# Rescaling a layer's normalized input in place, and three smaller edits, in a two-layer hybrid attention encoder

## The chip, the cores and the metric

The kernel runs on one core of one Trainium2 chip. A core has TensorE (PE in the profile, its weight loads PEld), VectorE (DVE), ScalarE (ACT), GpSimd (POOL) and SyncE (SP), which here only issues DMAs. They run their own instruction streams in order and wait for each other through semaphores. The metric is the device time of one execution in microseconds; the time before is the median of three runs.

## The reference

The input x is 512 tokens of 1024 numbers. Two layers follow, each of this form (D_MODEL is 1024, D_FF 2816):

```python
h = rms_norm(x, attn_norm_g[l])
proj = h @ w_in[l]
c_q, c_kv, k_rope, gq, gk, gv, pool_in, gate_logits = split_columns(proj, IN_SIZES)
o_mla = mla_branch(...)      # 8 heads of 96, low-rank q and kv
o_gqa = gqa_branch(...)      # 8 heads of 64 over 2 key/value heads
o_pool = pool_branch(...)    # centred means of windows 2, 4, 8, 16, minus the token
gates = sigmoid(gate_logits)
merged = (gates[:, :, 0] * (o_mla @ w_branch_mla[l])
          + gates[:, :, 1] * (o_gqa @ w_branch_gqa[l])
          + gates[:, :, 2] * (o_pool @ w_branch_pool[l]))
x = x + merged @ w_out[l]
hf = rms_norm(x, ffn_norm_g[l])
u = depthwise_conv(hf @ ffn_w_up[l], ...)
x = x + (silu(u_gate) * u_val) @ ffn_w_down[l]
```

`rms_norm(x, g)` is x times one factor of the token, 1/sqrt(mean(x*x) + eps), times one gain of the column. The attention branches normalize queries and keys per head once more, and take a softmax over 512 keys.

## The kernel before

**Layout.** The residual stream lies transposed in SBUF: `XM[:, kc]` holds 128 features (partitions) by 512 tokens, kc from 0 to 7. Each float32 matrix product is made of three float32r products (`mm3`, L396): every operand is kept as a high half (the number rounded to float32r) and a low half (what the rounding lost), and PE adds hi·hi, hi·lo and lo·hi in a PSUM bank. There are eight PSUM banks, handed out by tag: "acc", "S", "ST", "AV", "mi" (`ps`, `free`, L310 and L325).

**The normalized input.** `HH` and `HL` are the halves of x times the gain, *without* the token's factor. The norm's sums are made beside other work; `norm_finish` (L492) turns them into the token factors in two forms: `rt`, one number per partition for results whose partitions are tokens, and `rbc`, a 128x512 tile with the factor of each token along the free axis, for results whose partitions are features. Every product of HH and HL is scaled by one of them on the way out of PSUM.

**Order of a layer.** `tok_major` (L598) makes products with tokens on the partitions: four banks, one for each 128 tokens; for each kc one weight piece, 12 matmuls. `feat_major` (L615) makes products with features on the partitions, one bank, 24 matmuls for two weight pieces. A layer runs:
1. the MLA latents (`tok_major`, 384 columns), then the four groups of pool channels (`feat_major`), whose windowed sums run on POOL and DVE beside the next stages;
2. the GQA query projection (`tok_major(gqb, T)`, L772) into the banks `qtags` = AV, AV, mi, ST. Its results are squared by ACT (`gq_square`) and rotated by DVE (`gq_rope`, L786: three products from PSUM, the last into `gqr`, then the bank is free; the sum of the two parts is an addition of POOL's into `gqr`);
3. the projection of GQA keys, values and the MLA rotary key (`tok_major(kvb, 288, pool_product)`, L830). Ahead of its kc = 4, `pool_product` (L815) puts the four pool products into the same four banks `qtags`. `gk_evac` (L834) and `kv_evac` (L856) then take the results out, with ACT's `scale=rtok(b)` and DVE's product with `rtok(b)`;
4. GQA attention, with the gates and branch products of the pool branch and then of the GQA branch (`gates`, L902) put between the heads' matmuls as filler;
5. MLA attention, with the rest of the GQA and the MLA branches' gates and products as filler;
6. the output projection, the feed-forward layer (norm factor `rbc` on DVE, convolution on ACT and DVE), the down projection.

**Gates.** `gate(m)` makes 128 gate logits with `feat_major`; DVE multiplies the bank by `rbc` into a tile `gt` and frees the bank (`logits`), then ACT takes tanh(0.5 x) of that tile in place. `product` makes (tanh + 1) times the branch's bank; the merged sum gathers in XM.

**MLA softmax.** For a head, `a_part` (L1303) makes the four 128x512 blocks of scores of the leading halves and takes the maximum over each block's keys, in groups of 32 lanes (`largest`); `over_keys` takes it over the four blocks. The maxima of the four groups of 32 partitions then have to meet on one group: `gather` copies three 32x16 pieces there, from other partitions, into the tile `nmt`; `over_groups` reduces the four to `mrow`, negated; `row` multiplies it by a piece of the identity into 32 rows of `qb`, so that the next matmuls with `qb` as the moving operand (`b_part`, L1339) subtract each query's maximum inside PSUM. ACT's exponential follows, then its halves `ph` (ACT or DVE) and `pl` (DVE), and the products with the values.

**Weights.** SP streams the weights in 512 KB transfers into `raw`. `w_split` (L344) halves each piece of up to 512 columns: ACT copies to the high half, then the low half is raw minus high, on DVE for the first eight pieces, on POOL for the next three, and else on whichever `pick` (L367) finds earlier, with a bias of 2.54 us against DVE. The halves are made three pieces ahead of use (`LA`), in six buffers each.

**What sets the order.** All engines' programs are written out in an order that a planner inside the kernel decides at build time: `Clock` (L134 on) keeps a modelled time for PE and for each engine, `at` and `chain` put steps into a heap by modelled time, `done` and `need` carry the modelled due times, and the `Engine` wrappers (L215 on, the lines under which nearly all instructions of ACT, DVE and POOL are recorded) add each operation's modelled cost. So an added or a dearer operation can also shift the place of others. `low` lets a step of DVE give way for up to a given time while DVE has a backlog. On the chip each engine runs its list in that order, and a bank or buffer is waited for where the planner had expected it free.

The names of the profile: XM, HH, HL, `raw`, `wh`/`wl` (weight halves), `gqr` (rotated GQA queries), `gt` (gate tile), `nmt`, `mrow`, `qb` as above; `mxh` a pool group's mixed input; `kh` and `q` halves of keys and queries; `a`, `u` tiles of the feed-forward layer; `ps_TAG` a PSUM bank.

Of the kernel before, what the change touches and what calls it, by code (L numbers as in the profile page):

```python
# [18 lines left out]
P = 128  # L19
# [195 lines left out]
class Engine:  # L215
# [31 lines left out]

    def tensor_reduce(self, out, in_, *a, **k):
        self._two(in_)
        return self.eng.tensor_reduce(out, in_, *a, **k)  # L250

    def tensor_scalar(self, out, *a):
# [21 lines left out]
def trunk(ctx: ExitStack, tc: tile.TileContext, x, w, prm, gb, cst, pad, out):  # L274
# [57 lines left out]
    pieces, swidth = _stream()  # L332
    soff = np.concatenate([[0], np.cumsum(swidth)]) * P
    st = {"dma": 0, "split": 0, "use": 0}
    raws, halves = {}, {}

    def w_dma():
        i = st["dma"]
# [5 lines left out]
    def w_split():  # L344
        j = st["split"]
        sl, off, wd = pieces[j]
        while st["dma"] <= sl:
            w_dma()
        r = raws[sl][:, off:off + wd]
        hi = hlp.tile([P, T], F32R, tag="wh", name=f"wh{j}")  # L350
        lo = hlp.tile([P, T], F32R, tag="wl", name=f"wl{j}")
        ck.fin = ck.now
        if j == 0:
            V.tensor_copy(hi[:, :wd], r)
        else:
            A.activation(hi[:, :wd], r, AF.Copy)
        e = V if j < KC else G if j < KC + 3 else pick(W_BIAS, ck.fin + ck.SEM)
        ck.free[e.kind] = max(ck.free.get(e.kind, 0.0), ck.fin + ck.SEM)
        e.tensor_tensor(lo[:, :wd], r, f(hi[:, :wd]), ALU.subtract)
        done("w", j)  # L360
        if j + 1 == len(pieces) or pieces[j + 1][0] > sl:

            at(max(0.0, ck.free[e.kind] - ck.now) + D_FREE, lambda: w_upto(sl + 1 + RAW))
        halves[j] = (hi, lo)
        st["split"] += 1
# [193 lines left out]
    def layer(l, sq, xsrc):  # L559
# [35 lines left out]
            chain(([("rt", G1)], tables), after=20.0)  # L595


        def tok_major(banks, wd, between=None):  # L598
            for kc in range(KC):
                if between and kc == 4:  # L600
                    between()
                wh, wl = wnext()
                need(("H", G1, kc))
                if st["use"] <= 2:
                    late = ((HH, wl), (HL, wh)) if kc == 0 else ((HL, wh), (HH, wl))
                    for n, (x_, w_) in enumerate(((HH, wh), *late)):
                        for b in range(4):
                            mm(banks[b][:, :wd], x_[:, kc, b * P:b * P + P], w_[:, :wd], n == 0 and kc == 0, False)
                    continue
                for b in range(4):  # L610
                    bs = slice(b * P, b * P + P)
                    mm3(banks[b][:, :wd], HH[:, kc, bs], HL[:, kc, bs], wh[:, :wd], wl[:, :wd],
                        kc == 0, kc == KC - 1)

        def feat_major(acc, gen):  # L615

            for kc in range(KC):
                if kc:
                    yield
                if kc % 4 == 0:  # L620
                    wh, wl = wnext()
                need(("H", gen, kc))
                ws = slice((kc % 4) * P, (kc % 4) * P + P)
                mm3(acc, wh[:, ws], wl[:, ws], HH[:, kc, :], HL[:, kc, :], kc == 0, kc == KC - 1)

# [143 lines left out]
        at(0.5, set_keys)  # L769

        at(14.0, set_ones)
        tok_major(gqb, T)  # L772
        gqo = [slot("gqr") for _ in range(4)]

        def gq_square(b):
# [51 lines left out]

        ktags = ("acc", "acc", "S", "ST")
        kvb = [ps(t) for t in ktags]
        tok_major(kvb, 288, pool_product)  # L830
        gkn, kj, gk1 = slot("gkn"), slot("kj"), slot("gk1")
        krt = small("krt", [P, 4, 32], bufs=1)

        def gk_evac():  # L834
            for b in range(4):
                A.activation(gkn[:, b * P:b * P + P], kvb[b][:, 0:P], AF.Copy, scale=rtok(b))
            chain(*rope_steps(heads(gk1), heads(gkn), *(
                bc(tabs[1][:, o:o + 256].rearrange("p (b f) -> p b f", b=4)[:, :, None, :], [P, 4, 2, 64])
                for o in (0, 256)), [P, 4, 2, 64], 32, V), lambda: done("gkr", l), after=ck.fin - ck.now)
# [16 lines left out]
        def kv_evac(b):  # L856
            vh, v0 = VG[b]
            src = kvb[b][:, P:2 * P].rearrange("p (h f) -> p h f", f=64)
            A.activation(vh[:, :, 0:64], src, AF.Copy, scale=rtok(b))
            A.activation(krt[:, b, :], kvb[b][:, 2 * P:288], AF.Copy, scale=rtok(b))  # L860

            def lo():
                V.scalar_tensor_tensor(vh[:, :, 65:P], src[:, :, 1:64], rtok(b), f(vh[:, :, 1:64]), ALU.mult,
                                       ALU.subtract)
                V.scalar_tensor_tensor(v0, src[:, :, 0], rtok(b), f(vh[:, :, 0]), ALU.mult, ALU.subtract)
                free(ktags[b])
                done("vg", l, b)
            chain(lo, after=ck.fin - ck.now + 0.1)
# [33 lines left out]
        def gates(br, okey, odst, mode):  # L902
            hold = {}

            def gate(m):
                tag = "AV" if br == 2 and m < 2 else "acc"
                acc = ps(tag)
                yield from feat_major(acc, G1)
                t = hold[m] = slot("gt")

                def logits():
                    V.tensor_tensor(t[:, :T], acc, nrm["rbc"][:, :T], ALU.mult)
                    free(tag)

                chain(([("rbc", G1)], way(br, logits, 1.0)), lambda: A.activation(t[:, :T], t[:, :T], AF.Tanh, scale=0.5))

            def branch(m):
                acc = ps("acc")
# [248 lines left out]
        def attention(kind, fill, okey, odst):  # L1167
# [135 lines left out]
            def a_part(h, k):  # L1303
# [18 lines left out]
                def gather():  # L1322
                    for g in range(4):
                        if 32 * g != base:
                            V.tensor_copy(s["pk"][base:base + 32, g if g < 3 else base // 32], s["pk"][32 * g:32 * g + 32, 3])

                def over_groups():
                    V.tensor_reduce(s["row"][base:base + 32], s["pk"][base:base + 32].rearrange("p g j -> p j g"), AX.X, ALU.max,
# [283 lines left out]
        fb.upto(PRE_B)  # L1612
        while not ck.has(("tq", l, 0)) and fb.step():
            pass
        now_mla[0] = True
        attention("mla", fb, "om", omla)
        rest[0].finish()


        sq = slot("sq")  # L1620
# [307 lines left out]
```

## Time and profile before

| | |
|---|---|
| three runs | 1571.52 us median (1571.37 to 1576.09) |
| the profiled execution | 1572.05 us |
| its span (first to last instruction) | 1570.3 us |
| granted TensorE clock, mean | 0.999 |
| DMA | 166.46 MB, 106 GB/s on average |

The profile is of one execution. "Busy" is the time in which an engine executed instructions, as a share of the span or of a named stretch; semaphores and the issuing of DMAs do not count. In rows of groups, `out<-in 128x512 fp32r<-128x512 f32 x32` is the written and the read tile with their shapes and types and the number of instructions; numbers like `742/751/753` are the shortest, median and longest duration in ns; `| 15.3, 852 | 0.4` is the sum in us, the mean in ns, and the idle time of the engine just ahead of them. A row of a single instruction starts with its start time and its duration in us. A row of waits names the instruction that waited, behind the arrow the instruction that released it, and then the sum of the waits, their number and the longest, in us.

The layers' stages lie about here: GQA query projection at 44 to 66 us in the first layer and 826 to 848 in the second, the key/value projection right behind, GQA attention 130 to 240 (first layer), MLA attention 240 to 340 and 1020 to 1120, the output projection behind each of these, and the feed-forward layer with its evacuations `u` from about 443 us in the first layer; the down projection is last.

### The profile page before, as it was taken

Reading aid. Unit: us, or ns where it says so; the run is one execution under the profiler, and the core shown is the slowest. Engines: PE = TensorE matmul, PEld = TensorE weight load, DVE = VectorE, ACT = ScalarE, POOL = GpSimd, SP = SyncE. Lnnn points to the kernel's source line nnn. Section 1 sums busy time; section 2 is a strip of 40 time slices with the busy share of each in tenths; the row PEclk is TensorE's granted clock in tenths of the full one; section 3 lists DMA queues with packets and bytes.
Section 4 is the critical chain, followed back from the end, with each engine's and each line's share of the span. In section 5 each row is a group of like instructions: output and inputs, shape, how many; then the busy total and the mean of one; then the engine's idle time right before and its main releaser. Section 6 shows DMA issues by size and latency. Waiting matters only on the chain. (4 is left out here: it accounts for less than half of the span.)

```text
span 1570.3 us, 20451 instructions
## 1 busy us (share of the span) xinstructions
PE 1548.3 (99%) x7034; PEld 1288.0 (82%) x7034; DVE 1008.8 (64%) x1471; ACT 788.6 (50%) x1460; POOL 1032.4 (66%) x918
## 2 busy tenths in 40 slices
PE   9999999899999999999999999999999999999999
PEld 8878787778888888888898888877788888888888
DVE  6778889996267777711046788899862777776000
ACT  6557866664444444432244687756533444444221
POOL 4866986655667666654578669767546766666542
PEclk9999999999999999999999999999999999999999
DMA  5432234324323223333335222433252232332331
GB/s 201 126 113 74 75 111 141 101 91 136 106 94 100 100 97 94 94 120 109 114 106 135 93 79 70 147 116 112 69 157 98 86 102 94 96 100 99 108 129 46
DMA packets 82855, 166.46 MB, mean 106 GB/s; under 512 B 20928, under 2 KB 42944, under 8 KB 82752
## 3 DMA queue, kind: packets, MB, share of 16 engines
q1 hardware_dynamic: 82464, 165.03, 34.1%
q8 instruction: 55, 0.90, 0.2%
q14 instruction: 48, 0.39, 0.1%
q10 hardware_dynamic: 288, 0.14, 0.0%
HBM read 151.50 MB, written 13.63 MB: 105 GB/s over the span
## 5 line engine op out<-in xcount | busy, mean ns | idle before, releaser
L242 POOL TENSOR_TENSOR wl<-raw,wh 128x512 fp32r<-128x512 f32 (+2 forms) x499 | 671.0, 1356 | 356.5 <-ACT wh L235 331.6
L235 ACT ACTIVATE wh<-raw 128x512 fp32r<-128x512 f32 (+2 forms) x521 | 309.1, 607 | 122.7 <-PE ps_ST L389 41.3
L246 DVE SCALAR_TENSOR_TENSOR a<-u,prm,a 128x511 f32<-128x511 f32 x176 | 246.4, 1401 | 93.0 <-ACT a L235 86.1
L389 PE MATMUL ps_acc<-HH,wl 128*128 128x512 f32 x592 | 230.9, 390 | 0.4 <-POOL wl L242 0.4
L389 PE MATMUL ps_acc<-HH,wh 128*128 128x512 f32 x592 | 231.3, 391 | 0.0
L389 PE MATMUL ps_acc<-HL,wh 128*128 128x512 f32 x592 | 230.9, 390 | 0.0
L389 PEld LDWEIGHTS ps_acc<-HH,wl 128*128 128x128 f32 x592 | 111.3, 188 | 24.3 <-POOL wl L242 0.9
L389 PEld LDWEIGHTS ps_acc<-HH,wh 128*128 128x128 f32 x592 | 111.5, 188 | 22.9 <-issue 0.3
L389 PEld LDWEIGHTS ps_acc<-HL,wh 128*128 128x128 f32 x592 | 111.4, 188 | 22.9
L242 POOL TENSOR_TENSOR al<-a,ah 128x512 fp32r<-128x512 f32 x44 | 57.8, 1314 | 84.9 <-ACT ah L235 84.9
L389 PE MATMUL ps_AV<-HH,wh 128*128 128x512 f32 x288 | 112.3, 390 | 0.0
L389 PE MATMUL ps_AV<-HH,wl 128*128 128x512 f32 x288 | 112.1, 389 | 0.0
L389 PE MATMUL ps_AV<-HL,wh 128*128 128x512 f32 x288 | 112.1, 389 | 0.0
L389 PE MATMUL ps_ST<-HH,wh 128*128 128x512 f32 x240 | 93.5, 390 | 0.0
L389 PE MATMUL ps_ST<-HL,wh 128*128 128x512 f32 x240 | 93.4, 389 | 0.0
L389 PE MATMUL ps_ST<-HH,wl 128*128 128x512 f32 x240 | 93.4, 389 | 0.0
L235 ACT ACTIVATE ah<-a 128x512 fp32r<-128x512 f32 x44 | 27.8, 632 | 127.1 <-DVE a L242 127.1
L235 ACT ACTIVATE a<-a 128x512 f32<-128x512 f32 x44 | 27.8, 633 | 110.0 <-DVE a L246 110.0
L235 ACT ACTIVATE a<-u,prm 128x512 f32<-128x512 f32 x88 | 70.9, 808 | 20.8 <-DVE u L242 20.6
L235 ACT ACTIVATE HH<-XM,prm 128x512 fp32r<-128x512 f32 x32 | 23.1, 722 | 101.6 <-DVE XM L242 53.9
L235 ACT ACTIVATE gt<-gt 128x512 f32<-128x512 f32 x48 | 30.2, 630 | 75.5 <-DVE gt L242 73.3
L389 PEld LDWEIGHTS ps_AV<-HH,wl 128*128 128x128 f32 x288 | 54.1, 188 | 11.3
(415 smaller groups left out, 3798.4 us busy)
## 6 DMA issues: line engine op xcount, KB each, us to landing
raw<-w SPq DMA_DIRECT2D x228, 512.0 KB, 3.5
raw<-w SPq DMA_DIRECT2D x13, 384.0 KB, 3.0
XM<-x SPq DMA_DIRECT2D x16, 256.0 KB, 3.4
dtq<-tr SPq DMA_DIRECT2D x16, 192.0 KB, 1.9
dtk<-tr SPq DMA_DIRECT2D x16, 192.0 KB, 2.3
tf<-dtq SPq DMA_DIRECT2D x48, 64.0 KB, 2.3
tf<-dtk SPq DMA_DIRECT2D x48, 64.0 KB, 2.1
raw<-w SPq DMA_DIRECT2D x6, 448.0 KB, 3.4
```

Of the source, the lines that this page charges most:

```text
L235: return self.eng.activation(out, in_, func, **k)
L242: return self.eng.tensor_tensor(out, *a)
L246: return self.eng.scalar_tensor_tensor(out, *a)
L389: PE.matmul(o, lhsT=lhsT, rhs=rhs, start=start, stop=stop)
```

## The change

There are four edits.

- **The input gets the token factor in place.** `tok_major` takes a function that it calls behind each kc. During the GQA query projection it is `rescale(kc)`: once PE's 12 matmuls of that kc are issued, DVE makes hs = XM x gain x `rbc` (a new tile), ACT rounds hs into HH, and DVE puts hs - HH into HL, over the old halves. The key/value projection and the gates read these (`scaled=True` makes them wait for the "scaled" halves). `gk_evac` and `kv_evac` lose their factor.
- **The gates' tanh reads PSUM.** `logits` is gone; ACT takes tanh(0.5 x) straight from the bank into `gt` and the bank is freed behind that.
- **The shifted copies become reductions.** `gather` takes the maximum over an axis of one element instead of a copy. The planner's cost of a reduction with such a short axis (up to 4) grows by 0.08 us.
- **Weights' low halves.** During MLA attention `pick` is not asked; all low halves go to POOL.

```diff
     def tensor_reduce(self, out, in_, *a, **k):
         self._two(in_)
+        if in_.shape[-1] <= 4:
+            self.ck.took(self.kind, 0.08)
         return self.eng.tensor_reduce(out, in_, *a, **k)
...
-        e = V if j < KC else G if j < KC + 3 else pick(W_BIAS, ck.fin + ck.SEM)
+        e = V if j < KC else G if j < KC + 3 or pool_only[0] else pick(W_BIAS, ck.fin + ck.SEM)
...
-        def tok_major(banks, wd, between=None):
+        def tok_major(banks, wd, between=None, scaled=False, then=None):
...
-                need(("H", G1, kc))
+                need(("H", G1, kc, "scaled") if scaled else ("H", G1, kc))
...
+                if then:
+                    then(kc)
...
-        tok_major(gqb, T)
+        def rescale(kc):
+            hs_ = slot("hs")[:, :T]
+
+            def lo():
+                V.tensor_tensor(HL[:, kc], hs_, f(HH[:, kc]), ALU.subtract)
+                done("H", G1, kc, "scaled")
+
+            chain(([("rbc", G1)], lambda: V.scalar_tensor_tensor(
+                hs_, XM[:, kc], col(PRM_AG + kc), nrm["rbc"][:, :T], ALU.mult, ALU.mult)),
+                  lambda: A.activation(HH[:, kc], hs_, AF.Copy), lo, after=0.3)
+
+        tok_major(gqb, T, then=rescale)
...
-        tok_major(kvb, 288, pool_product)
+        tok_major(kvb, 288, pool_product, scaled=True)
...
-                A.activation(gkn[:, b * P:b * P + P], kvb[b][:, 0:P], AF.Copy, scale=rtok(b))
+                A.activation(gkn[:, b * P:b * P + P], kvb[b][:, 0:P], AF.Copy)
...
-            A.activation(vh[:, :, 0:64], src, AF.Copy, scale=rtok(b))
-            A.activation(krt[:, b, :], kvb[b][:, 2 * P:288], AF.Copy, scale=rtok(b))
+            A.activation(vh[:, :, 0:64], src, AF.Copy)
+            A.activation(krt[:, b, :], kvb[b][:, 2 * P:288], AF.Copy)
...
-                V.scalar_tensor_tensor(vh[:, :, 65:P], src[:, :, 1:64], rtok(b), f(vh[:, :, 1:64]), ALU.mult,
-                                       ALU.subtract)
-                V.scalar_tensor_tensor(v0, src[:, :, 0], rtok(b), f(vh[:, :, 0]), ALU.mult, ALU.subtract)
+                V.tensor_tensor(vh[:, :, 65:P], src[:, :, 1:64], f(vh[:, :, 1:64]), ALU.subtract)
+                V.tensor_tensor(v0, src[:, :, 0], f(vh[:, :, 0]), ALU.subtract)
...
-                yield from feat_major(acc, G1)
+                yield from feat_major(acc, G1, scaled=True)
                 t = hold[m] = slot("gt")
 
-                def logits():
-                    V.tensor_tensor(t[:, :T], acc, nrm["rbc"][:, :T], ALU.mult)
+                def squash():
+                    A.activation(t[:, :T], acc, AF.Tanh, scale=0.5)
                     free(tag)
 
-                chain(([("rbc", G1)], way(br, logits, 1.0)), lambda: A.activation(t[:, :T], t[:, :T], AF.Tanh, scale=0.5))
+                chain(squash)
...
-                            V.tensor_copy(s["pk"][base:base + 32, g if g < 3 else base // 32], s["pk"][32 * g:32 * g + 32, 3])
+                            V.tensor_reduce(s["pk"][base:base + 32, g if g < 3 else base // 32],
+                                            s["pk"][32 * g:32 * g + 32, 3].unsqueeze(2), AX.X, ALU.max)
...
-        now_mla[0] = True
+        now_mla[0] = pool_only[0] = True
         attention("mla", fb, "om", omla)
         rest[0].finish()
+        pool_only[0] = False
```

In instructions: PE's are the same in number, and in the same order up to GQA attention. DVE gets 16 hs and 16 HL, loses the 48 products of the gates, has 48 reductions in place of the copies, and eight instead of thirteen of the weights' 512-column low halves; POOL has five more of these. ACT gets 16 copies into HH. SP's transfers are the same in number and order.

More of the change, by code (lines that the diff above doesn't have):

```diff
@@ L334, in trunk @@
     st = {"dma": 0, "split": 0, "use": 0}
-    raws, halves = {}, {}
+    raws, halves, pool_only = {}, {}, [False]
     def w_dma():
@@ L613, in tok_major, with feat_major @@
                         kc == 0, kc == KC - 1)
-        def feat_major(acc, gen):
+                if then:
+                    then(kc)
+        def feat_major(acc, gen, scaled=False):
             for kc in range(KC):
@@ L621, in feat_major @@
                     wh, wl = wnext()
-                need(("H", gen, kc))
+                need(("H", gen, kc, "scaled") if scaled else ("H", gen, kc))
                 ws = slice((kc % 4) * P, (kc % 4) * P + P)
```

## The prediction

> **What bounds the kernel now.** I read the page's busy table first, then waits of PE, then stretches of 20 to 100 us, then single instructions.
>
> ```profile
> span 1570.3 us, 20451 instructions
> ...
> PE 1548.3 (99%) x7034; PEld 1288.0 (82%) x7034; DVE 1008.8 (64%) x1471; ACT 788.6 (50%) x1460; POOL 1032.4 (66%) x918
> ```
>
> TensorE (PE) is the bound: 22 us of the span are not matmul time, and the change leaves every matmul in place. So only PE's waits can be won, and every new one is lost in full. The profiled execution took 1572.05 us, 1.75 around its span and 0.03% over the median of 1571.52; the sum below starts from 1572.05.
>
> ```profile
> 240.00:340.00 100.00, 93.17 (x401) 74.13 (x400) 98.10 (x162) 61.82 (x116) 65.91 (x56) 1.00 0.37 111
> 340.00:440.00 100.00, 100.00 (x443) 82.64 (x442) 48.47 (x68) 44.13 (x79) 57.84 (x45) 1.00 0.38 116
> 1020.00:1120.00 100.00, 92.19 (x391) 73.84 (x391) 97.67 (x159) 58.44 (x110) 66.26 (x55) 0.98 0.35 107
> 1100.00:1120.00 20.00, 18.10 (x73) 14.50 (x72) 18.93 (x30) 9.77 (x19) 11.26 (x11) 0.91 0.23 75
> 44.00:66.00 22.00, 22.00 (x98) 17.94 (x97) 10.95 (x22) 8.95 (x20) 18.94 (x18) 1.00 0.64 155
> 826.00:848.00 22.00, 22.00 (x100) 18.29 (x99) 10.97 (x21) 6.88 (x14) 17.41 (x19) 1.00 0.61 150
> 57.96:68.33 10.37, 10.34 (x52) 8.46 (x51) 6.29 (x12) 6.09 (x13) 7.53 (x7) 1.00 0.65 137
> 834.58:847.84 13.26, 13.26 (x61) 11.00 (x60) 5.54 (x13) 6.72 (x14) 9.47 (x9) 1.00 0.64 144
> 130.00:240.00 110.00, 108.80 (x501) 89.71 (x501) 96.11 (x179) 82.12 (x161) 86.97 (x117) 1.00 0.31 93
> ```
>
> Columns: stretch, length, busy time and count of PE, PEld, DVE, ACT, POOL, granted clock, DMA. The first and third rows are MLA attention of the two layers. There DVE is 98% busy and PE issues 401 and 391 matmuls per 100 us against 443 at full rate (second row): 42 and 52 missing, 9.5 and 11.7 us, together 21.2. The fourth row shows a part of it: a granted clock of 0.91 over 20 us, 1.8 us.
>
> ```profile
> PE ps_ST L1348 <- DVE qb L242: 6.8, 4, 1.9
> PE ps_AV L1348 <- DVE qb L242: 4.8, 4, 1.9
> ...
> PE ps_S L393 <- ACT gt L235: 1.1, 1, 1.1
> ```
>
> PE's longest waits are for qb, the row of negated maxima. One of them, by DVE, POOL and PE:
>
> ```profile
> 1086.35 3.46 DVE L258 COPY nmt<-nmt 32x16 f32<-32x16 f32 x3
> 1089.85 0.26 DVE L250 TENSOR_REDUCE mrow<-nmt 32x16 f32<-32x64 f32 x1
> 1090.21 0.69 DVE L242 TENSOR_TENSOR qb<-mrow,C 32x512 fp32r<-32x512 f32 x1
> ...
> 1088.50 1.28 POOL L242 TENSOR_TENSOR wl<-raw,wh 128x512 fp32r<-128x512 f32 x1
> ...
> 1090.95 0.50 PE L1348 MATMUL ps_ST<-qb,kh 128*128 128x512 f32 x1 [1.84 <-DVE qb L242]
> ```
>
> Three copies of 16 elements take 3.46 us and end (1089.81) when POOL's subtraction ends (1089.78); a reduction of 64 elements takes 0.26. PE stands 1.84 us behind them.
>
> **Part 1, MLA attention: copies, gates, weights.**
>
> ```profile
> L258 DVE COPY nmt<-nmt 32x16 f32<-32x16 f32 x18 | 15.3, 852 | 0.4
> ...
> L242 DVE TENSOR_TENSOR gt<-ps_acc,rbc 128x512 f32<-128x512 f32 x7 | 4.7, 675 | 0.0
> ...
> L242 DVE TENSOR_TENSOR wl<-raw,wh 128x512 fp32r<-128x512 f32 x2 | 2.4, 1178 | 0.1
> ```
>
> (DVE, 240 to 340 us.) A reduction over one element replaces each copy. None of 32x16 inputs is in the trace; its price lies between 0 and the 0.26 of the four times larger one; I take 0.26. DVE then sheds 18 x (0.852 - 0.26) = 10.7, all gates' products 4.7 and the weights' halves 2.4: from 98.1 to about 80 us. A head's chain to qb shrinks by 3 x 0.59 = 1.8 on average, by 2.7 in the case shown, as much as PE waits there. What is late next is the usual exp and its halves, which filler matmuls cover. I take **-20** of the 21.2; bounds -10 (half stays) and -21.
>
> The weights' halves that leave DVE (five of 512 in the program) cost POOL 1.3 us each; POOL is at 66% there: 0, and 1.3 each if a weight is just due.
>
> **Part 2, gates.** The tanh reads the accumulator; 48 DVE products vanish.
>
> ```profile
> L235 ACT ACTIVATE gt<-gt 128x512 f32<-128x512 f32 x48 | 30.2, 630 | 75.5 <-DVE gt L242 73.3
> ```
>
> ACT keeps 48 instructions of about this length; reading PSUM instead of SBUF is not shown for tanh, so I keep 0.63. The accumulator is now freed by ACT instead of DVE. Behind a tanh that waits stand exponentials and weights' halves, for which PE waits; ACT is 62% busy in MLA, 82 of 110 us in GQA (last row of stretches), so 0, and 0.63 for a gate if ACT is late. GQA has 1.2 us of PE idle; with DVE lighter I take **-1** (0 to -1.2).
>
> **Part 3, the rescale.** Per layer and per kc it adds hs (DVE, from XM and rbc), a copy to HH (ACT), HL (DVE). Per layer 16 DVE and 8 ACT instructions enter beside the GQA projection. No transfer is added, and SP keeps its order.
>
> ```profile
> L246 DVE SCALAR_TENSOR_TENSOR HL<-XM,prm,HH x32: 742/751/753, 4.9 to 1208.3; 128x512 fp32r<-128x512 f32 x32
> ...
> L242 DVE TENSOR_TENSOR XM<-XM,gt x16: 692/1084/1796, 366.2 to 1165.7; 128x512 f32<-128x512 f32 x16
> L242 DVE TENSOR_TENSOR mgl<-XM,mgh x16: 691/692/694, 367.6 to 1168.2; 128x512 fp32r<-128x512 f32 x16
> ```
>
> Alone, hs costs 0.75 and HL 0.69, mean 0.72. With two operands in SBUF, an addition can take up to 1.80. What waits is queued behind them: the rope of the GQA queries, which frees the four PSUM banks of the pool products, which PE issues in the middle of the next projection. In the changed program's order seven HL and five hs come between the first layer's 57.96 us and its first rope (68.33), two more before the last rope; in the second layer 13 between 834.58 and 847.84, then two.
>
> ```profile
> 73.38 0.68 DVE L242 TENSOR_TENSOR gqr<-ps_ST,tabg 128x512 f32<-128x512 f32 x1
> ...
> 74.67 0.39 PE L389 MATMUL ps_ST<-mxh,wh 128*128 128x512 f32 x1
> ...
> 852.89 0.68 DVE L242 TENSOR_TENSOR gqr<-ps_ST,tabg 128x512 f32<-128x512 f32 x1
> ...
> 855.94 0.39 PE L389 MATMUL ps_ST<-mxh,wh 128*128 128x512 f32 x1
> ```
>
> The last bank is freed 0.61 us (74.67 - 74.06) and 2.37 us before PE takes it. DVE's idle time in the two stretches is 10.37 - 6.29 = 4.08 and 13.26 - 5.54 = 7.72. First layer: 14 x 0.72 - 4.08 - 0.61 = 5.4 late. Second: 15 x 0.72 - 7.72 - 2.37 = 0.7. Floor: **6.1**.
>
> Above it comes POOL, busy 18.94 and 17.41 of 22 us, 83%. Some seven of the new instructions of a layer meet it; afterwards POOL's next instruction is the addition into gqr, which waits for the rope. A random arrival waits half of a subtraction: 0.83 x 0.65 = 0.54, 14 times 7.6. DVE's wait for ACT's copy between hs and HL (0.63) is spent in the same gaps. I take 6.1 + 7.6 = **+14**; bounds 6 and 24 (each of the 14 waits for all 1.29 of a subtraction: 18.1).
>
> The Trainium skill, "SBUF — State Buffer", section "Who interferes with whom", says that a DVE instruction with two SBUF inputs and a GpSimd instruction that reads SBUF block each other for the whole instruction, and that a reduction never contends on trn2. The additions of up to 1.80 agree, the reductions of 0.26 too; by the full block the term would be the upper bound, the first rival.
>
> PE's 1.1 us wait in the first layer (ps_S, listed under ACT) falls behind the new one: **-1**. The other edits (evacuations without a factor) swap forms of one length: 0.
>
> **Sum:** -20 - 1 - 1 + 14 = -8: 1572.05 - 8 = **1564 us**, 0.5% under the median.
>
> **The rivals.**
>
> *Lock-step in the GQA projection (slower).* DVE and POOL alternate, each new instruction pays a whole subtraction, weights come late too: 24. PE's standstills then cost clock as in the row with 0.91, 1.8 us a layer: 27.8. Sum -22 + 27.8 = +6: 1578. It outweighs the gain from a term of 22, a wait of (22 - 6.1) / 14 = 1.14 us each. For it: POOL's share, and additions at 1.80. Against it: POOL runs out of work before the rope.
>
> The skill's "TensorE: Matmul & The Clock Gate", "Part 1: The HAM clock gate", has half clock after an idle window of about 3.4 us; one standstill per layer of 5 us or more would bring it.
>
> *No contention.* The new instructions fall between POOL's: 6 instead of 14, 1556. Against it: 83%.
>
> *MLA is not cleared.* The replaced copies wait as before, or another wait takes their place (ACT's copies, kh from DMA): gain 10 instead of 20: 1574. Against it: 0.26 for a reduction beside POOL, and DVE's fall to 80%.
>
> **How the numbers follow.** Chances: forecast 0.44 (own range 1557 to 1570), lock-step 0.38, no contention 0.10, MLA not cleared 0.08. About 0.3%, 4.7 us, is what a measurement can tell from no change: 1566.8 to 1576.2 is "same". Faster: 0.34 of the forecast and 0.10; same: 0.10 of it, 0.08, and 0.02 of lock-step; slower: 0.36. The range runs from 1553 (no contention, all of MLA and GQA cleared) to 1583 (lock-step with 15 of the 20 won).
>
> **What would show it.** Right: nmt reductions under 0.3 us beside POOL, MLA stretches with 440 matmuls per 100 us and DVE near 80%, PE idle before the pool products of 5 to 9 us a layer, released by DVE gqr. Wrong: no idle there, or over 11 us a layer with a granted clock under 1; waits for qb that stay; a new wait of PE for an accumulator that ACT holds.

## The result and the profile after

The changed kernel takes 1583.57 us, median of five runs (1581.72 to 1585.15), against 1571.37 for the kernel before (five runs in all): a ratio of 1.0076, 95% interval 1.0057 to 1.0096. It is 12 us slower, where 1564 and a gain of 8 had been forecast; the time lies 0.6 us over the top of the range. The profiled execution, 1585.15 us, has a span of 1583.4 us, 13.1 over that of before.

From the page of the changed kernel:

```profile
span 1583.4 us, 20454 instructions
...
PE 1554.8 (98%) x7034; PEld 1293.4 (82%) x7034; DVE 986.6 (62%) x1447; ACT 797.8 (50%) x1480; POOL 1045.2 (66%) x922
```

DVE is lighter by 22 us, and PE waits more. Where it waits is in the stretches of the changed kernel (stretch, length, busy time and count of PE, PEld, DVE, ACT, POOL, granted clock, DMA):

```profile
240.00:340.00 100.00, 100.00 (x445) 82.91 (x444) 90.44 (x171) 66.80 (x126) 78.02 (x68) 1.00 0.47 137
1020.00:1120.00 100.00, 100.00 (x448) 82.99 (x447) 90.09 (x171) 67.77 (x128) 79.54 (x68) 1.00 0.47 143
...
130.00:240.00 110.00, 106.19 (x484) 86.77 (x483) 86.84 (x154) 84.16 (x166) 86.15 (x118) 1.00 0.23 73
920.00:1020.00 100.00, 96.01 (x436) 78.03 (x435) 77.92 (x138) 77.20 (x151) 77.16 (x105) 1.00 0.23 69
60.00:80.00 20.00, 14.73 (x74) 11.30 (x73) 17.99 (x28) 9.61 (x18) 8.59 (x8) 1.00 0.35 86
80.00:100.00 20.00, 16.84 (x83) 14.38 (x82) 19.38 (x37) 11.47 (x31) 15.79 (x15) 0.83 0.32 99
848.00:880.00 32.00, 25.29 (x127) 21.02 (x126) 29.20 (x49) 17.32 (x33) 22.85 (x20) 0.89 0.31 88
```

MLA attention (first two rows) is clear: PE is busy all of the time, with 445 and 448 matmuls per 100 us. GQA attention (next two) is not: 3.8 and 4.0 us without a matmul, where the first had 1.2 before. The projections (last three) lose most: PE is busy 14.73 of 20 us, and behind that its granted clock is 0.83.

The waits of PE in the changed kernel (released by, sum, times, longest):

```profile
PE ps_acc L391 <- POOL wl L242: 4.8, 8, 0.7
PE ps_S L391 <- DVE nm L252: 2.9, 2, 1.5
PE ps_acc L391 <- DVE vm L242: 2.7, 2, 1.4
PE ps_AV L391 <- DVE gqr L242: 2.6, 2, 1.3
PE ps_mi L391 <- DVE gqr L242: 2.0, 2, 1.0
PE ps_acc L391 <- ACT wh L235: 1.8, 2, 1.3
PE ps_ST L391 <- POOL qb L242: 1.8, 4, 0.7
PE ps_ST L391 <- ACT oph L235: 1.7, 2, 0.9
PE ps_AV L391 <- ACT wh L235: 1.4, 1, 1.4
...
PE ps_AV L391 <- POOL wl L242: 0.9, 1, 0.9
```

DVE's qb, the longest wait before, is gone. In its place stand the weights' halves (wl and wh, 8.9 us in all), the ropes' banks (gqr, and the last of the four, listed under oph, 6.3 us), and in GQA attention nm, vm and POOL's qb.

For the comparisons below the waits are added up by stage, so that half clock and restarts count too: for each matmul, the distance to the start of the next one minus the median distance for its shape (0.227 us for 512 columns). This is worked out from the matmuls' starts in each trace; the sums are us of one profiled execution, "1" and "2" are the layers, and stages are cut at the same places of PE's work. A 0 stands for -0.2 to 0.1. GQA attention here begins right behind the projections; the "3 and 1 us" of the expectations are for 130 to 240 us and 920 to 1020 us alone.

```
                                     span  projections    GQA att.      MLA att.
                                             1     2       1     2       1     2
before                             1570.3   0.6   0.3     5.7   1.0     9.5  11.6
after                              1583.4  14.2  11.8     7.4   7.7     0     0
e1  no rescale, no gates' edit     1553.1   0.6   0.2     4.4   1.9     2.1   2.1
e2  gates' edit, no rescale        1559.1   0.6   0.5     8.9   6.9     0     0
e3  rescale, no gates' edit        1574.5  11.6  10.5     3.3   1.0     2.1   3.7
e4  after, no copy to HH           1578.8  11.8   9.1     7.4   7.9     0     0
e5  after, POOL quiet              1559.9   2.6   1.8     7.1   6.9     0     0
e6  after, rescale in kv           1582.9   6.0  13.0    15.2   7.0     0     0
e7  e2 in the order of e1          1557.5   0.6   0.2     5.5   2.9     3.3   3.3
e8  reductions alone               1562.4   0.6   0.5     4.5   1.0     7.1   6.9
e9  after, GQA's halves on POOL    1570.6  11.8   9.8     3.7   3.3     0     0
e10 e1 with more filler            1549.6   0.6   0.5     4.5   1.0     0.5   0.6
e11 MLA's halves on POOL alone     1569.5   0.6   0.3     4.4   1.0    10.8  10.8
e12 e9, no rescale                 1550.6   0.6   0.5     3.8   3.3     0     0
```

After minus before: -21.3 in MLA attention (the prediction's first term said -20), +25.1 in the projections (+14), +8.4 in GQA attention (-2 for the gates and the keys' wait together), 0.8 at the start.

### The profile page after: what moved, and what is told of

It is laid out like the page before. It is cut to its first block, busy times and chain, and to the rows that moved or that the text cites. A ratio compares the mean times of both kernels' runs of the same rounds, so it can differ in the third digit from the quotient of the medians.

```text
span 1583.4 us, 20454 instructions
## 1 busy us (share of the span) xinstructions
PE 1554.8 (98%) x7034; PEld 1293.4 (82%) x7034; DVE 986.6 (62%) x1447; ACT 797.8 (50%) x1480; POOL 1045.2 (66%) x922
## 4 chain that ended last, share of the span: by engine, by line
PE 86%; DVE 4%; POOL 4%; ACT 3%; issue 2%; DMA 1%; SPq 0%; POOLq 0%; DVEq 0%; ACTq 0%
PE ps_acc L391 40%; PE ps_AV L391 21%; PE ps_ST L391 19%; PE ps_S L391 2%; PE ps_mi L391 2%; POOL wl L242 1%; DVE hs L246 1%; PE ps_ST L1363 1%; POOL oraw L242 1%; DMA XM<-x 1%; DVE wl L242 1%; ACT wh L235 1%; POOL qa L242 0%; PE ps_ST L1321 0%; DMA raw<-w 0%
## 5 line engine op out<-in xcount | busy, mean ns | idle before, releaser
L242 POOL TENSOR_TENSOR wl<-raw,wh 128x512 fp32r<-128x512 f32 (+2 forms) x503 | 678.0, 1360 | 398.4 <-ACT wh L235 361.2
L235 ACT ACTIVATE ah<-a 128x512 fp32r<-128x512 f32 x44 | 27.8, 632 | 129.1 <-DVE a L242 129.1
L235 ACT ACTIVATE a<-a 128x512 f32<-128x512 f32 x44 | 27.8, 632 | 105.6 <-DVE a L246 105.5
L391 PEld LDWEIGHTS ps_AV<-HH,wh 128*128 128x128 f32 x288 | 54.1, 188 | 11.5 <-DVE sq L242 0.4
```

The costliest lines, as they stand in the source:

```text
L235: return self.eng.activation(out, in_, func, **k)
L242: return self.eng.tensor_tensor(out, *a)
L391: PE.matmul(o, lhsT=lhsT, rhs=rhs, start=start, stop=stop)
```

## The experiments

Four kernels first crossed the two doubtful edits, with the reductions and the weights' rule in all of them: neither the rescale nor the gates' edit (e1), the gates' edit alone (e2), the rescale alone (e3), both (the changed kernel). The programs of PE are equal in e1 and e3, and in e2 and the changed kernel, so that the rescale can be read off without a change of order.

**e1**: the changed kernel without `rescale`, with the gates' `logits` and the evacuations' factors as before.

```diff
+            V.tensor_reduce(s["pk"][base:base + 32, g if g < 3 else base // 32],
+                            s["pk"][32 * g:32 * g + 32, 3].unsqueeze(2), AX.X, ALU.max)
...
+        e = V if j < KC else G if j < KC + 3 or pool_only[0] else pick(W_BIAS, ck.fin + ck.SEM)
```

> The kernel before with the two edits of MLA attention alone: reductions in place of the shifted copies, all low halves of the weights on POOL there. No rescale; the gates' logits stay a DVE product. Theory P (the prediction's sum): these two edits win -20 in MLA attention and nothing else moves, 1571.4 - 20 = 1551 us, and PE's lost time in GQA attention (130 to 240 us and 920 to 1020 us) stays at 3 and 1 us as before. Rival (the whole gain needs the lighter DVE of the gates as well): 1558 or more, with waits for qb of over 5 us left.

Measured: 1555.23 us (1554.72 to 1557.40) beside 1570.12 for the kernel before, ratio 0.9907 (0.9892 to 0.9922). The two small edits win 15 us; the waits for qb are gone, GQA attention is as before. The 4 us that are missing to 1551 are at the end of each MLA stage, a wait for `vt`, which e8 and e10 take up.

**e2**: e1 with the gates' tanh from PSUM; HH and HL unscaled.

```diff
-                def logits():
-                    V.tensor_tensor(t[:, :T], acc, nrm["rbc"][:, :T], ALU.mult)
+                def squash():
+                    A.activation(t[:, :T], acc, AF.Tanh, scale=0.5)
                     free(tag)
```

> e1 plus the gates' tanh from PSUM, with HH and HL left unscaled: the token factor is left out of the gates' logits. PE's program is that of the changed kernel, without the rescale's instructions. Theory P (tanh from PSUM costs nothing; the GQA attention's new loss of 10.7 us comes from the lateness that the rescale brings): 1550 us, GQA attention as in e1. Theory Q (the loss belongs to the gates' edit: the planner's other order of PE, DVE and ACT, with the tanh in ACT's queue): 1551 + 10 = 1561 us, with the waits for DVE nm and DVE vm in GQA attention also here.

**e3**: the changed kernel with the gates' `logits` back on DVE, as in the kernel before.

> The changed kernel with the gates' logits on DVE as before: they are multiplied by the token factor a second time. PE's program is that of e1. Theory P: as the changed kernel, 1583, the GQA attention's loss of 10 us is here too. Theory Q: 1583.6 - 10 = 1573 us, GQA attention at 3 and 1 us lost as in e1, the projection's 11 us per layer unchanged.

Measured: e2 1559.25 us (1558.92 to 1560.85), ratio 0.9929 (0.9913 to 0.9946); e3 1576.72 (1576.29 to 1578.06), ratio 1.0043 (1.0028 to 1.0058); same chip as e1. Theory Q holds and P falls: the loss of GQA attention is in e2, without any rescale, and not in e3, with all of it. The edits' prices nearly add: the rescale costs 1576.7 - 1555.2 = 21.5 us, the gates' edit 1559.3 - 1555.2 = 4.0, so 1580.7 with both, where the ratio of the changed kernel, 1.0076, gives 1582.1 on this chip. The 4.0 are a balance: by the table e2 loses 9.5 us more than e1 in GQA attention, and wins back e1's 4.2 in MLA attention.

**e4**: the rescale without ACT's copy.

```diff
-                  lambda: A.activation(HH[:, kc], hs_, AF.Copy), lo, after=0.3)
+                  lo, after=0.3)
```

> The changed kernel without ACT's copies of hs into HH (the high halves stay unscaled, the low halves are hs minus those). DVE's instructions are all there; ACT never waits for hs, and the weights' high halves aren't queued behind such a wait; DVE doesn't wait for ACT between hs and HL. Theory A (the DVE instructions alone, each waiting for POOL, make the ropes late and PE waits for the pool products' banks): PE's loss in the two projections stays at 11 to 12 us a layer, 1582 to 1584, now all of it ahead of the pool products. Theory B (ACT's in-order queue: HH waits for hs and the next weights' halves stand behind it): the loss falls to 6 us a layer or less, 1573 or less, and the waits for wh and wl at 63 to 79 us are gone.

Measured: 1580.59 us (1580.37 to 1580.83), ratio 1.0066 (1.0051 to 1.0081). The waits of PE in e4:

```profile
PE ps_AV L391 <- DVE gqr L242: 4.8, 4, 2.6
...
PE ps_mi L391 <- DVE gqr L242: 3.1, 2, 1.6
...
PE ps_acc L391 <- ACT wh L235: 2.0, 2, 1.1
...
PE ps_acc L391 <- POOL wl L242: 1.2, 2, 0.6
```

With the shorter waits, which are not listed here, those for weights shrink from 8.9 to 3.6 us, and those for the ropes' banks grow from 6.3 to 8.4: the projections lose 11.8 and 9.1 us instead of 14.2 and 11.8. ACT's queue decides for the most part where PE stands, and for a smaller part how long. That is theory A in the main (its time was put at 1582 or more, and not all of the waiting stands at the ropes), with some 2.5 us a layer for B.

**e5**: POOL's subtractions of the two projections' weights become memsets.

```diff
+        if e is G and 16 <= j % PER < 33:
+            G._two(lo[:, :wd])
+            nc.gpsimd.memset(f(lo[:, :wd]), 0.0)
+        else:
             e.tensor_tensor(lo[:, :wd], r, f(hi[:, :wd]), ALU.subtract)
```

> The changed kernel, but the low halves of the GQA and key/value projections' weights (pieces 16 to 32 of each layer) are set to zero by a POOL memset in the place of the subtraction; that part of these products is left out. The programs of PE, DVE and ACT are those of the changed kernel. Theory K (DVE's instructions with two SBUF operands wait for POOL's subtractions): hs falls from a mean of 1.41 us to under 1.0, HL to 0.7, and PE's loss in the two projections from 14 and 12 us to under 6 each, 1570 or less. Theory L (32 more instructions are too many for DVE's gaps whatever POOL does, and DVE and ACT wait for each other): hs gets shorter, but 9 us or more a layer stay, 1576 or more.

Measured: 1561.69 us in one run, beside 1572.74 for the kernel before on that chip. DVE's new instructions in the changed kernel, then in e5 (shortest, median, longest in ns):

```profile
L246 DVE SCALAR_TENSOR_TENSOR hs<-XM,prm,rbc x16: 740/1285/1793, 50.7 to 864.8; 128x512 f32<-128x512 f32 x16
L242 DVE TENSOR_TENSOR HL<-hs,HH x16: 674/692/1779, 58.6 to 867.7; 128x512 fp32r<-128x512 f32 x16
```

```profile
L246 DVE SCALAR_TENSOR_TENSOR hs<-XM,prm,rbc x16: 740/746/1555, 49.0 to 844.8; 128x512 f32<-128x512 f32 x16
```

Theory K: with POOL's reads of SBUF out of the way hs takes 0.75 us instead of 1.29 in the median, the projections lose 2.6 and 1.8 us, and with the same 32 instructions of DVE the rescale costs 2 to 3 us in all (e5 against e2: 1561.7 to 1559.3 on different chips, 4.4 to 1.1 us lost in the projections). The Trainium skill, "SBUF — State Buffer", section "Who interferes with whom", says that a DVE instruction with two SBUF inputs contends with a GpSimd instruction that reads SBUF and not with one that only writes it. The memsets agree with it: the median of 0.75 is that of an undisturbed instruction. The price belongs to the two together: POOL's subtractions without the rescale (e2) lose 0.6 and 0.5 us in the projections, the rescale without the subtractions 2.6 and 1.8, both 14.2 and 11.8. What e5 can't tell apart is DVE's relief from that of PE, for which the memsets also come earlier than the subtractions.

**e6**: the rescale one stage later, behind the key/value projection's kc, which reads the unscaled halves again.

```diff
-        tok_major(gqb, T, then=rescale)
+        tok_major(gqb, T)
...
-        tok_major(kvb, 288, pool_product, scaled=True)
+        tok_major(kvb, 288, pool_product, then=rescale)
```

> The changed kernel with the rescale one stage later: behind each kc of the key/value projection, which again reads the unscaled halves and has its token factors at the evacuations. Same number of instructions (the evacuations' forms apart). Theory N (the price is DVE time in a stretch where DVE is full, wherever it is put between the query projection and the gates): the ropes are in time, but the keys' evacuation and the first gates come late, the loss is as large, 1580 or more. Theory M (the price comes from the ropes that free the pool products' banks, and from the weights' halves of the short pieces): the loss in both projections falls to under 5 us a layer, 1570 or less.

Measured: 1586.02 us (1584.65 to 1588.55), ratio 1.0079 (1.0054 to 1.0104): theory N. The longest waits of PE in e6:

```profile
PE ps_AV L391 <- DVE HL L242: 11.4, 2, 5.7
PE ps_ST L391 <- DVE gqr L242: 6.2, 2, 3.6
```

Moved off the query projection, the rescale is waited for by the first gate, 5.7 us in each layer (in the table this wait is counted with GQA attention in the first layer, with the projections in the second). The ropes are not in time either, as theory N had them: their last bank is waited for 3.6 and 2.6 us. A place a stage later is no cheaper.

**e7**: e2, but the planner goes on counting a DVE product per gate, so that PE and POOL have the programs of e1.

```diff
                 def logits():
-                    V.tensor_tensor(t[:, :T], acc, nrm["rbc"][:, :T], ALU.mult)
+                    V._two(t[:, :T])
                     free(tag)
...
-                chain(([("rbc", G1)], way(br, logits, 1.0)), lambda: A.activation(t[:, :T], t[:, :T], AF.Tanh, scale=0.5))
+                chain(([("rbc", G1)], way(br, logits, 1.0)), lambda: A.activation(t[:, :T], acc, AF.Tanh, scale=0.5))
```

> e2 with the planner's books left as they were: it still counts a DVE product for each gate and frees the modelled bank behind it, but the product isn't issued and tanh reads PSUM (the token factor is left out of the gates). PE's and POOL's programs are those of e1. Theory O (the 4 us of e2 over e1 come from the order that the planner writes for GQA attention): as e1 or slightly faster, 1553 to 1556, PE's loss in GQA attention 3 and 1 us. Theory Q2 (a tanh in ACT's queue that holds the bank is dear by itself): 1558 or more, with waits for a bank that ACT holds.

Measured: 1558.98 us (1558.05 to 1559.33) beside 1572.74, ratio 0.9902 (0.9876 to 0.9928), which includes e1's 0.9907. For GQA attention theory O holds in the main: 5.5 and 2.9 us, near e1's 4.4 and 1.9 and not e2's 8.9 and 6.9. The time itself is undecided, since 3.3 us are lost in each MLA stage, against 2.1 in e1. Part of that is a wait for the branch's product (first row). The sign of theory Q2 is there too, but small: PE waits twice in GQA attention, 1.1 us in all, for a bank that ACT's tanh holds (second row).

```profile
PE ps_acc L391 <- DVE gt L246: 2.9, 2, 1.4
...
PE ps_acc L391 <- ACT gt L235: 1.1, 2, 0.7
```

**e8** and **e11**: the two small edits apart. e8 is the kernel before with the reductions only, e11 with the weights' rule only.

> The kernel before with the reductions in place of the shifted copies alone; weights in MLA attention go where the planner puts them. If the copies were the whole of MLA's loss: 1555 as e1, the wait for vt of 1.4 us at the end of each MLA stage perhaps gone. If the low halves on POOL are needed as well: 1560 or more, with waits for qb or weights left in MLA attention.

> The kernel before with the weights' low halves in MLA attention on POOL alone, copies as before. If the copies that wait for POOL hold PE up, relieving DVE of five low halves wins nothing: 1570 to 1572, the waits for qb stay at 13 us. If DVE's load was the cause: 1566 or less.

Measured: e8 1563.40 us (1562.29 to 1564.56) beside 1572.74, ratio 0.9931 (0.9904 to 0.9958); e11 1574.04 (1571.30 to 1577.56) beside 1572.05, ratio 1.0009 (1.0000 to 1.0019). The waits of PE in e8, then in e11:

```profile
PE ps_AV L391 <- DVE vt L246: 3.5, 2, 1.7
...
PE ps_ST L1351 <- DVE qb L242: 0.2, 1, 0.2
```

```profile
PE ps_AV L1348 <- DVE qb L242: 5.9, 4, 2.3
PE ps_acc L389 <- DVE gt L246: 3.8, 4, 1.9
PE ps_S L1348 <- DVE qb L242: 2.8, 3, 2.0
```

e11 is as its first theory said in the main: relief of DVE's load alone wins nothing. (Its waits for qb come to 10 us and not to 13, with longer ones for gt.) e8 met neither expectation: the copies were all of the waits for qb (0.2 us are left), but the time is at 1563, with a new loss at the end of each MLA stage. PE's program suggests why: between the last head's scores and its last product there are 21 filler matmuls in the kernel before, 9 in e1 and none in e8.

**e10**: e1 with more of the MLA branch's gates as filler.

```diff
-SOONER = {1: 3 * KC, 0: 6 * KC}
+SOONER = {1: 3 * KC, 0: 52}
```

> e1 with 52 instead of 48 units of the MLA branch's gates as filler in MLA attention; the same work in another place. In e1 9 filler matmuls are left between the last head's scores and its last product, 21 in the kernel before; here it is 24. If the 1.7 us that e1 loses at the end of each MLA stage are filler that ran out: 1555.2 - 3.4 = 1552, the wait for vt gone. If the filler is missed elsewhere: 1555 or more.

Measured: 1551.72 us (1551.39 to 1553.97) beside 1572.05, ratio 0.9872 (0.9855 to 0.9888). The losses at the stage's end are gone, so in e1 they were filler that ran out; for e8 the same is likely, but no run gave it more filler. This is the fastest kernel of the study, 1.3% faster than the one before and, by the two ratios, 2.0% faster than the changed one. From its page:

```profile
PE 1542.4 (100%) x7034; PEld 1287.8 (83%) x7034; DVE 983.7 (63%) x1469; ACT 789.0 (51%) x1458; POOL 1040.7 (67%) x922
```

**e9**: the changed kernel with the weights' rule in GQA attention too.

```diff
+        pool_only[0] = True
         attention("gqa", fa, "og", ogqa)
```

> The changed kernel with all of the weights' low halves on POOL in GQA attention as well. In GQA attention DVE then has none of the four low halves a layer, two of which (1.4 and 1.7 us beside POOL) stand ahead of the maximum nm that PE waits for. Theory R (these cause the loss there): PE's lost time in GQA attention falls from 6.3 and 6.0 us to 4 or less each, 1578 or less. Rival S (POOL, 86 of 110 us busy, is late in its place, with the rows qb and the weights): 6 us or more stay in each layer, 1582 or more, with longer waits for POOL qb or POOL wl.

Measured: 1574.98 us (1572.21 to 1576.58, ten runs) beside 1572.05, ratio 1.0018 (1.0008 to 1.0027). Theory R: GQA attention loses 3.7 and 3.3 us. What stood in the way can be seen in the changed kernel, in time order (start, duration):

```profile
209.81 1.47 POOL L242 TENSOR_TENSOR MQ<-MQ,ssm 128x768 f32<-128x768 f32 x1
...
210.13 0.39 PE L391 MATMUL ps_S<-ka,qa 128*128 128x512 f32 x1
...
210.15 1.69 DVE L242 TENSOR_TENSOR wl<-raw,wh 128x512 fp32r<-128x512 f32 x1
...
211.75 0.74 DVE L246 SCALAR_TENSOR_TENSOR vt<-ps_mi,vg,vt 128x512 fp32r<-128x512 f32 x1
...
212.42 0.68 DVE L252 TENSOR_REDUCE nm<-ps_S 128x1 f32<-128x512 f32 x1
...
213.15 0.51 PE L391 MATMUL ps_S<-ka,qa 128*128 128x512 f32 x1 [1.46 <-DVE nm L252]
```

DVE starts a weight's subtraction at 210.15, which ends at 211.84, half a microsecond behind POOL's MQ (211.28); the maximum nm comes behind it, and PE waits 1.46 us for the bank that nm reads.

**e12**: e9 without the rescale.

> e9 without the rescale (e2 with all low halves on POOL in GQA attention too): the token factor is left out of the gates' logits. It shows what the gates' edit is worth at best, when nothing is given back in GQA attention and the rescale costs nothing. By the losses of e9, whose projections lose 20 us more than before: 1575 - 20 = 1555 from its median, 1550.6 + 1.8 = 1552 from its profiled execution. Theory U (once the reductions have cleared MLA attention, PE has almost nothing left that a lighter DVE could win): no better than e10's 1551.7 by more than 1.5 us. Rival V (the lighter DVE is worth something by itself): 1549 or less.

Measured: 1552.40 us (1551.60 to 1553.03) beside 1571.82, ratio 0.9873 (0.9857 to 0.9890), the same as e10. Theory U: with the reductions in place, the gates' edit at its best wins nothing that filler does not win too.

## Why the prediction was wrong, point by point

Of the 21 us by which the profiled execution missed the sum, 11 lie in the rescale and 10 in GQA attention.

**The copies, -20: right in size, only in part for the reason given.** MLA attention gave back 21.3 us. The copies before:

```profile
L258 DVE COPY nmt<-nmt x48: 167/982/1316, 234.4 to 1120.1; 32x16 f32<-32x16 f32 x48
```

What replaces them in the changed kernel:

```profile
L252 DVE TENSOR_REDUCE nmt<-nmt x64: 161/163/270, 250.4 to 1132.0; 32x16 f32<-32x16 f32 x48, 128x16 f32<-128x64 f32 x16
```

A move takes 0.16 us, less than the 0.26 that was taken. The shortest copy took 0.17 as well, so most of the others' 0.98 was a wait. DVE stands at 90% of the stretch and not at 80 because the stretch now holds more work: for the 401 matmuls of before it is 90.44 x 401/445 = 81.5 us. The prediction took copies, gates and weights together as the relief; e8 and e11 show that the waits for qb were the copies' own, and that the rest is how the planner spreads filler. In that the size is partly luck: two of the three edits gave back 16.9 us (e1), the gates' edit the last 4.2 by another order, and e10 gets most of these with filler alone.

**The rescale, +14: contention right, its size and part of the path wrong.** The step that failed is "Some seven of the new instructions of a layer meet it", with the price behind it, "A random arrival waits half of a subtraction: 0.83 x 0.65 = 0.54, 14 times 7.6". Of the 32 new instructions of both layers 17 were lengthened, 14 of the 16 hs and three HL, by 0.75 us on average, 12.8 in all. At 0.54 for each of the 32 the rule gives 17.3, more than came: the count was too small, not the price of a random arrival. The reason for the seven was that POOL then runs out of work and itself waits for the rope. POOL is indeed busy only 8.59 of the 20 us from 60, but its idle time lies between the weights' subtractions, which wait for ACT's wh (1.69 us at 860.35 below), and five of the six hs that start there are lengthened beside one of these. The second layer of the changed kernel, in time order:

```profile
859.31 0.63 ACT L235 ACTIVATE HH<-hs 128x512 fp32r<-128x512 f32 x1 [1.59 <-DVE hs L246]
...
859.85 0.43 ACT L235 ACTIVATE wh<-raw 128x288 fp32r<-128x288 f32 x1
...
859.97 0.69 DVE L242 TENSOR_TENSOR HL<-hs,HH 128x512 fp32r<-128x512 f32 x1
...
860.35 0.96 POOL L242 TENSOR_TENSOR wl<-raw,wh 128x288 fp32r<-128x288 f32 x1 [1.69 <-ACT wh L235]
860.58 1.28 DVE L246 SCALAR_TENSOR_TENSOR hs<-XM,prm,rbc 128x512 f32<-128x512 f32 x1
...
861.37 0.40 PE L391 MATMUL ps_acc<-wl,HH 128*128 128x288 f32 x1 [0.64 <-POOL wl L242]
...
861.96 0.63 ACT L235 ACTIVATE HH<-hs 128x512 fp32r<-128x512 f32 x1 [1.68 <-DVE hs L246]
...
862.50 0.43 ACT L235 ACTIVATE wh<-raw 128x288 fp32r<-128x288 f32 x1
...
862.62 0.69 DVE L242 TENSOR_TENSOR HL<-hs,HH 128x512 fp32r<-128x512 f32 x1 [0.76 <-ACT HH L235]
```

In these rows ACT sets the two engines going together. Its copy to HH releases DVE's HL; ACT then makes wh, which releases POOL's wl; so wl and the next hs start within 0.23 us of each other, and hs (1.28 us) ends 0.55 behind wl's end at 861.31. Its end releases the next copy to HH. One turn takes 861.96 - 859.31 = 2.65 us, and PE, whose 12 matmuls of a kc take 12 x 0.13 = 1.6, waits for wl, 0.64 us here. A turn this short comes once in each layer; with a rope or a window sum in between it is longer.

This loop makes PE wait for weights, but the collisions do not need it. In e4 ACT makes no HH, and hs and HL wait for nothing of ACT's:

```profile
L246 DVE SCALAR_TENSOR_TENSOR hs<-XM,prm,rbc x16: 737/1284/1782, 50.8 to 862.3; 128x512 f32<-128x512 f32 x16
L242 DVE TENSOR_TENSOR HL<-hs,HH x16: 685/1184/1594, 52.1 to 864.2; 128x512 fp32r<-128x512 f32 x16
```

There the 32 take 36.6 us, in the changed kernel 17.5 and 18.3 in the two layers, 35.9 together (summed over the single instructions of the traces). Why the two meet as often there, without the loop, stays open.

In the sum, 12.8 in the place of 7.6 gives 6.1 + 12.8 = 18.9 of the 20.7 us that the rescale cost without the clock (below). The upper bound, a whole subtraction for each of the 14, was 18.1; the 12.8 lie halfway between it and 7.6. This is a sum of DVE's time and not PE's path: more than half of what PE waits for in the projections are the weights' halves (8.9 us, against 6.3 at the ropes' banks), which the forecast put at nothing and left to the lock-step rival. e4 shows that without them PE stands longer before the ropes' banks instead, 8.4 us. The floor of 6.1 held contention too: in e5 the term falls under it, and the window sums, one of which takes 1.74 us instead of 0.69 in the same stretch of the changed kernel, run at 0.69.

**The clock, 1.8 a layer in the lock-step rival: present, and not in each execution.** The row with 0.83 above has half clock around the last ropes. In e9's profiled execution, whose programs are the same up to there, the stretch has

```profile
80.00:100.00 20.00, 16.78 (x94) 14.10 (x93) 19.62 (x38) 12.06 (x33) 15.87 (x15) 1.00 0.37 124
```

11 matmuls more in as much busy time. The projections of the two executions differ by 2.4 and 2.0 us, so by this one pair the rescale without the clock is 20.7 of the 25.1.

**The gates, 0 and -1: wrong in sign.** The step that failed is "with DVE lighter I take **-1** (0 to -1.2)", beside the cost of 0 for a tanh that reads PSUM. GQA attention lost 8.4 us more than before. ACT's queue was not the trouble: no wait of PE for a bank that ACT's tanh holds stands in the changed kernel. The freed time of DVE was given away: in the planner's books DVE was free sooner, `pick` put weights' subtractions there at places where PE's next bank hangs on DVE, and each of them has two SBUF operands and mostly costs 1.4 to 1.7 us beside POOL:

```profile
L242 DVE TENSOR_TENSOR wl<-raw,wh x4: 684/1478/1687, 196.8 to 223.4; 128x512 fp32r<-128x512 f32 x3, 128x256 fp32r<-128x256 f32 x1
```

The kernel before has four of these in GQA attention as well, at other places. That e7 and e12 (the old order, and no pick) lose 3.4 to 5.1 us less than e2 in each layer's GQA attention, and e9 3.7 and 4.4 less than the changed kernel, shows it. In the second layer e9 and e12 still lose 3.3 us where the kernel before lost 1.0; this remainder is not explained. The prediction had compared the planned orders for the projections but priced GQA attention from the order of before.

**PE's 1.1 us wait in the first layer: right.** It is in the 5.7 of before and gone in the changed kernel.

**SP's order: stated wrongly.** SP's transfers are the same in number but not in order: in the changed program nine of them, of weights and stores of queries, stand a few places elsewhere. No wait of PE for a transfer showed up.

**The range.** Its top was lock-step with 15 of MLA attention's 20 us won. The rescale's 25.1 us came near lock-step's 27.8, though by shorter waits than the whole subtractions that it supposed, and with all 21 won; the loss of GQA attention, which lay outside of every case, carried the time past the top. The bottom, 1553, is not what its terms give: 1572.05 - 21.2 - 1.2 - 1 + 6.1 = 1554.8.

## What to carry to other kernels

Work that is added to an engine takes its price from every one of its instructions that can meet another engine's, not only from those ahead of the one wait that was looked at, and a low busy share of the other engine is no safeguard: here five of six hs were lengthened in a stretch in which POOL was busy 43% of the time. The waits that come with it can also stand elsewhere, here at the weights' halves behind ACT's queue. Time that an edit frees on an engine goes where the planner sends it, so the plan behind the edit has to be read for what now stands in the freed place. And once the wait that bounds a stage is gone, further relief there is worth nothing: here the replacing of 48 small copies, with the weights and the filler fitted to it, won 1.3%, and the rescale that was to make the gates lighter cost 1.4% for a gain that was no longer to be had.

## What the runs showed of the hardware

Half clock came without a long standstill. In the changed kernel the longest single wait of PE is 1.5 us; before the dip it was busy 2.83 of 6 us:

```profile
866.00:872.00 6.00, 2.83 (x9) 1.55 (x9) 6.00 (x13) 4.38 (x9) 5.42 (x5) 0.88 0.41 137
872.00:878.00 6.00, 6.00 (x26) 5.71 (x26) 5.93 (x10) 2.56 (x5) 6.00 (x7) 0.55 0.28 85
```

The second row is at a clock of 0.55: by the clock's records half clock lasts 6.83 us from 870.51, and as long from 85.45 in the first layer. In the 3.41 us ahead of each PE was busy 1.69 us, and its longest wait was 1.3. All such dips in the traces of before, e3, e4, e6, e8 and e11 last 3.41 or 6.83 us too, and in the 3.41 us ahead of each PE was busy 1.9 us or less. In e9's first layer nearly the same waits brought no dip, so what decides it is not shown. The prediction drew on the Trainium skill's idle window of 3.4 us and a standstill of 5 us. The Trainium skill's "TensorE: Matmul & The Clock Gate" has a nearer case in its section "A second HAM failure mode: psum-queue depth-cycling": many short waits between groups of matmuls let the clock fall back as well. The rows agree with that one. The ten runs of e9 show what it is worth: 1572.2 and 1572.4 us at a mean granted clock of 1.000, 1574.5 to 1576.6 at 0.995 to 0.998.

A reduction over one element takes 0.16 us beside a busy POOL, where the copy of the same 32x16 elements took 0.98 in the median: the same move of data, in a form that does not wait.
